# Two branch projections moved from the attention loop into the gate stage, and the values as a Strassen product

## The chip, the cores and the metric

The kernel runs on one core of one Trainium2 chip. The metric is the device time of one execution in microseconds; the median of three runs of the kernel before is 1399.12 us (1399.05 to 1400.21).

## What is computed

A decoder block for x of 1024 positions by 1024 channels, float32. The part that matters here, cut from the reference:

```python
h = rmsnorm(x, attn_norm_g[l])
z = h @ w_in[l]                          # u, v (512) | pooling (256) | q, k (1024) | values (512)
gates = jax.nn.sigmoid(h @ w_gate[l] + b_gate[l])      # 3 x 1024 columns
y_a = gmlp_mixer(z[..., :o_a], ...)      # layer norm of v, spatial gating, 256 channels
y_b = pool_mixer(z[..., o_a:o_b], ...)   # causal means over 2, 4, 8, 16 positions, 256 channels
y_c = diff_attn_mixer(...)               # 4 heads, two softmaxes each, 512 channels
merged = g_a * (y_a @ proj_a[l]) + g_b * (y_b @ proj_b[l]) + g_c * (y_c @ proj_c[l])
x = x + merged @ w_out[l]
x = x + conv_ffn(rmsnorm(x, ffn_norm_g[l]), w_up[l], conv_w[l], conv_b[l], w_down[l])
return rmsnorm(x, final_norm_g)
```

## The kernel before

Each float32 operand is split into a high part (a cast, L96 on ScalarE) and a low part (a subtraction, L97 on VectorE), both of a type that TensorE multiplies in one pass, and each product of two operands is three matmuls, high by low, high by high and low by high (`mm3`, L187 to L190). L189 is the line of nearly all matmuls. An activation is held as eight tiles of 128 channels by 1024 positions.

Most projections go through `strassen_pair` (L251 to L289): two output tiles of 128x1024, F1 and F2, from seven products (Strassen in Winograd's form) of 12 matmuls of 128x512 each, 84 in place of 96. `prepare` (L224) loads the weights and forms the operand sums on POOL; `winograd` (L209) forms the sums of the activation. Each result is an add on VectorE of a PSUM bank and a copied partial result (L260). The argument `mid` is called at four points of a pair, so that other work may be put between its products. The PSUM pool p1 has six banks with the tag "b" for these products and two with the tag "m" (`pm1`) for small work.

The stages in order, with their times in the profile:

- 0 to 61 us: RMS norm and the projections u and v.
- 61 to 118 us: `values` (L496), eight groups of 48 matmuls of 128x256, with `layer_norm`, `gating` and the `winograd` sums of h written between them.
- 118 to 200 us: one pair for the pooling branch, zb, and pairs for q and k of heads 0 to 2. `pooling` (L529) works on zb in steps that are called from the `mid` of the pairs; `pool_out` (L572) is a small matmul on its result. `times_r` (L347) multiplies a tile by the row factors RB, on POOL unless told otherwise. `store_qk` splits and stores q and k.
- 200 to 448 us: twelve gate pairs (loop at L689). Of each result POOL does `times_r`, ScalarE the sigmoid (L694), and the tile is stored to g_d.
- to 455 us: the pair of the last head's q and k.
- 455 to 604 us: attention, a loop over 32 tiles (head, block of 128 queries) in four steps that work on tiles t to t-3: scores (L677, L678, PE) with a running maximum (L680, VectorE), the exponential (L686, ScalarE), `combine` of the two softmaxes (L1003 to L1005, VectorE), transposition (L1020, PE), its copy (L1021, ScalarE) and the product with the values (L1029, PE). The generator `merge_ab` (L1086) is the filler of this loop: in each tile one group of 12 matmuls (mm<-yv,ph), a projection of y_a or y_b, and its product on VectorE with the sigmoid gate, read back from g_d as ga or gb (L1096). `load_p` splits the projection weights ph, `load_yab` the tiles yv.
- 604 to 1398 us: `merge_c`, the output projection, the FFN, the last norm.

A tile scheduler sets the order of the instructions of each engine from a simulated timeline when the program is built; each engine runs its queue in that order. SBUF tiles come from pools of a fixed number of buffers: a4 (34), w4 (13), c2 (6).

## Time and profile before

| What | us |
|---|---|
| median of three runs | 1399.12 |
| profiled execution | 1400.12 |
| its span on the core | 1398.4 |
| PE busy | 1349.2 (96%) |
| VectorE (DVE) busy | 958.0 (69%) |
| ScalarE (ACT) busy | 646.3 (46%) |
| GpSimd (POOL) busy | 516.8 (37%) |
| mean granted TensorE clock | 0.991 |

A busy time is a sum over the whole span; what a change in one stage is worth is read from the windows of that stage. A group of instructions in a view reads: line, engine, operation, tile written <- tiles read, form, count, then busy time and mean length, then the idle time of the engine before them and who ended it.

### The profile page before, as it was taken

To read this page: it belongs to the slowest core of one execution; us is meant where nothing else is said; L and a number is where in the kernel's file an instruction comes from. 1 tells how busy PE (TensorE), PEld (TensorE's weight loads), DVE (VectorE), ACT (ScalarE), POOL (GpSimd) and SP (SyncE) were. 2 spreads that over 40 slices of the span, in tenths; PEclk is the share of its full clock that TensorE was granted. 3 is DMA by queue.
4 is the path that set the end of the run, shared out by engine and by line. 5 is a ranking of instruction groups with operands and counts; after the bars stand their busy time and mean duration, and the time that the engine had idled before them with its cause. 6 is when DMAs were issued, how large, how long until landed. Compare 5 with 4: busy or idle time off the path is not lost.

```text
span 1398.4 us, 17778 instructions
## 1 busy us (share of the span) xinstructions
PE 1349.2 (96%) x6502; PEld 1126.8 (81%) x6502; DVE 958.0 (69%) x1464; ACT 646.3 (46%) x1105; POOL 516.8 (37%) x333
## 2 busy tenths in 40 slices
PE   8999999999999889999999999999999999999996
PEld 7898778888887678878777888888888887878786
DVE  7654766444454789967869677666777668985854
ACT  8542335343334567732666343433433435455461
POOL 0023376465552100012231566666666640102014
PEclk9999999999999999999999999999999999999998
DMA  6432235233338898497795222222222247845853
GB/s 204 131 97 77 76 151 181 91 120 106 113 114 233 254 239 233 130 268 180 207 229 121 91 75 90 78 74 90 90 76 90 81 161 271 286 120 152 224 129 121
DMA packets 79407, 204.65 MB, mean 146 GB/s; under 512 B 8334, under 2 KB 17678, under 8 KB 79320
## 3 DMA queue, kind: packets, MB, share of 16 engines
q1 hardware_dynamic: 67800, 180.44, 39.3%
q0 software_dynamic: 11520, 23.07, 9.5%
q8 instruction: 51, 0.84, 0.3%
q14 instruction: 36, 0.29, 0.1%
HBM read 143.70 MB, written 47.46 MB: 137 GB/s over the span
## 4 chain that ended last, share of the span: by engine, by line
PE 66%; DMA 11%; DVE 11%; issue 4%; ACT 3%; POOL 2%; SPq 0%; DVEq 0%; POOLq 0%; ACTq 0%
PE b L189 59%; PE mm L189 2%; DMA fr<-in_w_out 2%; DMA x<-in_xT 2%; PE ms L1029 1%; DMA fr<-in_w_down 1%; DVE fw L97 1%; DMA r<-in_w_gate 1%; DVE Sl L97 1%; DMA qs<-qk_d 1%; DMA pr<-in_w_proj 1%; POOL F L349 1%; DMA ssb<-sq 1%; DVE ft L97 1%; PE at L1020 1%
## 5 line engine op out<-in xcount | busy, mean ns | idle before, releaser
L189 PE MATMUL b<-ft,fw 128*128 128x512 f32 (+1 forms) x1308 | 291.8, 383 | 8.8 <-DVE fw L97 3.1
L189 PEld LDWEIGHTS b<-ft,fw 128*128 128x128 f32 x1308 | 238.9, 188 | 59.0 <-DVE fw L97 4.4
L349 POOL TENSOR_TENSOR F<-F,RB 128x1024 f32<-128x1024 f32 x74 | 205.3, 2777 | 135.3 <-DVE F L260 133.5
L189 PE MATMUL b<-hb,Ah 128*128 128x512 f32 x608 | 189.0, 390 | 0.0
L260 DVE TENSOR_TENSOR F<-b,c 128x512 f32<-128x512 f32 x152 | 100.6, 682 | 99.8 <-ACT c L279 46.5
L189 PE MATMUL b<-T,Sh 128*128 128x512 f32 x504 | 155.7, 389 | 2.0 <-ACT c L270 2.0
L97 DVE TENSOR_TENSOR Sl<-s,Sh 128x1024 fp32r<-128x1024 f32 x76 | 118.1, 1554 | 28.7 <-ACT Sh L96 20.8
L232 POOL TENSOR_TENSOR s<-r 128x512 f32<-128x512 f32 x36 | 56.7, 1576 | 207.4 <-DMA r<-in_w_up 83.4
L189 PEld LDWEIGHTS b<-hb,Ah 128*128 128x128 f32 x608 | 114.0, 188 | 23.9 <-issue 0.5
L97 DVE TENSOR_TENSOR Al<-r,Ah 128x1024 fp32r<-128x1024 f32 x38 | 51.6, 1358 | 102.7 <-issue 75.5
L189 PE MATMUL b<-hb,Al 128*128 128x512 f32 x304 | 118.4, 389 | 2.5 <-DVE Al L97 2.5
L96 ACT CAST Sh<-s 128x1024 fp32r<-128x1024 f32 x76 | 80.0, 1052 | 72.2 <-PE b L189 46.3
L189 PEld LDWEIGHTS b<-T,Sh 128*128 128x128 f32 x504 | 94.6, 188 | 21.9 <-ACT c L270 2.4
L189 PE MATMUL b<-hb,Sh 128*128 128x512 f32 x304 | 95.1, 394 | 4.0 <-DVE F L260 4.0
L189 PE MATMUL b<-T,Sl 128*128 128x512 f32 x252 | 98.1, 389 | 0.0
L96 ACT CAST Ah<-r 128x1024 fp32r<-128x1024 f32 x38 | 39.9, 1050 | 108.1 <-PE b L189 108.1
L96 ACT CAST fw<-fr 128x512 fp32r<-128x512 f32 x90 | 54.9, 623 | 62.2 <-DVE fw L97 26.3
L189 PE MATMUL b<-Tl,Sh 128*128 128x512 f32 x204 | 79.4, 389 | 0.0
L189 PE MATMUL b<-Th,Sl 128*128 128x512 f32 x204 | 78.7, 390 | 0.1
L189 PE MATMUL b<-Th,Sh 128*128 128x512 f32 x204 | 78.6, 389 | 0.0
L189 PE MATMUL b<-wh,hb 128*128 128x256 f32 x384 | 71.9, 286 | 1.9 <-ACT vg L425 1.9
L189 PEld LDWEIGHTS b<-hb,Sh 128*128 128x128 f32 x304 | 57.6, 190 | 16.9 <-DVE F L260 4.9
(250 smaller groups left out, 2802.6 us busy)
## 6 DMA issues: line engine op xcount, KB each, us to landing
fr<-in_w_down SPq DMA_DIRECT2D x47, 512.0 KB, 4.0
r<-in_w_up SPq DMA_DIRECT2D x42, 512.0 KB, 3.5
r<-in_w_gate SPq DMA_DIRECT2D x24, 512.0 KB, 3.8
g_d<-F SPq DMA_DIRECT2D x24, 512.0 KB, 2.6
act_d<-cv SPq DMA_DIRECT2D x22, 512.0 KB, 2.6
act<-act_d SPq DMA_DIRECT2D x22, 512.0 KB, 6.9
fr<-in_w_out SPq DMA_DIRECT2D x18, 512.0 KB, 5.7
ssb<-sq POOLq DMA_DIRECT2D x24, 256.0 KB, 3.9
```

The source lines that it names most:

```text
L96: nc.scalar.copy(hi, src)
L97: (eng or nc.vector).tensor_tensor(out=lo, in0=src, in1=hi.bitcast(F32), op=ALU.subtract)
L189: nc.tensor.matmul(ps, lhsT=w[a], rhs=x[b], start=first and i == 0, stop=last and i == 2, skip_group_check=more)
L232: eng.tensor_tensor(out=s1[:, :NH], in0=a21, in1=a22, op=ALU.add)
L260: nc.vector.tensor_tensor(out=o, in0=ps, in1=c, op=ALU.add)
L349: (eng or nc.gpsimd).tensor_tensor(out=F, in0=F, in1=RB, op=ALU.mult)
L1020: nc.tensor.transpose(pt[:, b * P:(b + 1) * P], st[t]["pr"][0][:, (4 * g + b) * P:(4 * g + b + 1) * P], ident)
L1029: nc.tensor.matmul(po[:, :P], lhsT=AH[t][:, kb, :], rhs=H["V"][:, kb, :], start=kb == 0, stop=kb == i)
```

## The change

Four things change.

- The values become one Strassen product: seven products of 48 matmuls of 128x256 where there were eight groups of 48. All `winograd` sums of h are formed ahead of it, the weights are loaded raw, and their sums and splits are made on VectorE and ScalarE between the products.
- `gating` and `pool_out` are tied in the order to the last matmul written before them; `pooling` takes two steps per `mid` and is finished within the first q/k pair; `pool_out` goes into the third. `times_r` of q and k of heads 0 to 2 goes to VectorE.
- The projections of branches a and b leave attention. `branch` computes them for gate pair n in the `mid`s of pair n+1, for the eight pairs of gates a and b, into the two "m" banks, and multiplies by the sigmoid tile in SBUF; F2 comes before F1. g_d then holds products, and `load_mg` reads and sums two of them with an accumulating DMA, from tile 20 of attention on. The attention loop has no filler; scores get four PSUM banks instead of three.
- `start` in the third part of `strassen_full` runs under a raised priority, and five of the eight scalings in the tail read PSUM instead of a copy.

```diff
-    def load_V(c):
-        return [list(load_parts(w_tm[1 + c, j].rearrange("p a b -> p (a b)"), 2, True))[0] for j in range(2)]
+    def load_V():
+        r = [[w4(n="wr") for _ in range(2)] for _ in range(2)]
+        for c, k in ((0, 0), (0, 1), (1, 0), (1, 1)):
+            nc.sync.dma_start(out=r[c][k], in_=w_tm[1 + c, k].rearrange("p a b -> p (a b)"))
+        return r
...
-    def values(c, gs):
...
+    def values():
+
+        (a11, a12), (a21, a22) = w_V
...
+        def prod(banks, w, tn, first, more):
+            for t in range(4):
+                for j in range(4):
+                    x, y = [o[:, t * P:(t + 1) * P] for o in h.T[j][tn]], wsl(w, j, 256)
+                    dst = banks[t // 2][:, t % 2 * 256:t % 2 * 256 + 256]
...
+                        mm3(dst, x, y, False, j == 3, True)
...
+        def store(o, banks, c, r, i):
+
+            for b in range(2):
+                TT(out=o[b], in0=banks[b], in1=c[b], op=ALU.add)
+                for t in range(2):
+                    sl = o[b][:, t * 256:(t + 1) * 256]
+                    nc.scalar.mul(sl, sl, R8[:, 4 * i + 2 * b + t:4 * i + 2 * b + t + 1])
...
+        A11, A12 = operand(a11), operand(a12)
+        b1, b2 = ([pb1() for _ in range(2)] for _ in range(2))
+        prod(b1, A11, "B11", True, True)
+        c1 = copies([c2("v") for _ in range(2)], b1)
+        yield
+        s1, s2 = w4(n="s1"), w4(n="s2")
+        TT(out=s1, in0=a21, in1=a22, op=ALU.add)
+        TT(out=s2, in0=s1, in1=a11, op=sub)
+        prod(b2, A12, "B21", True, False)
+        store(c1, b2, c1, 0, 0)
+        S1 = operand(s1)
+        yield
+        b3 = [pb1() for _ in range(2)]
+        prod(b3, S1, "T1", True, True)
+        S2 = operand(s2)
+        TT(out=a21, in0=a11, in1=a21, op=sub)
+        TT(out=a12, in0=a12, in1=s2, op=sub)
+        yield
+        prod(b1, S2, "T2", False, True)
+        k2 = copies(wide("c2"), b1)
+        S3 = operand(a21)
+        yield
+        prod(b1, S3, "T3", False, True)
+        k3 = copies(wide("c3"), b1)
+        store([c2("v") for _ in range(2)], b3, k3, 1, 1)
+        A22 = operand(a22)
+        yield
+        b4 = [pb1() for _ in range(2)]
+        prod(b4, A22, "T4", True, False)
+        store(k3, b4, k3, 1, 0)
+        S4 = operand(a12)
+        yield
+        prod(b3, S4, "B22", False, True)
+        store(k2, b3, k2, 0, 1)
...
+            with tc.issue_after(last_mm[0].ins):
+                for c in range(2):
+                    ch = 2 * g + c
+                    nc.tensor.matmul(pv[:, c], lhsT=vg[ch // 4][:, ch % 4, f * P:(f + 1) * P],
...
-    values(0, (2, 3))
-    h.winograd(xt, 0)
+    for j in range(4):
+        h.winograd(xt, j)
+    vs = values()
+    next(vs)
     layer_norm()
-    values(1, (2, 3))
-    h.winograd(xt, 1)
-    values(0, (0, 1))
-    h.winograd(xt, 2)
+    for _ in range(4):
+        next(vs)
     gating(0)
-    values(1, (0,))
+    next(vs)
     gating(1)
-    h.winograd(xt, 3)
     wB = prepare(w_qk[0])
-    values(1, (1,))
+    next(vs)
     zb = strassen_pair(wB, h, pb1)
...
+    def pool_outs():
+        for f in range(2):
+            yield
+            with tc.issue_after(last_mm[0].ins):
+                pool_out(f, zb[f])
+
     for i in range(NHEAD - 1):
         ops = prepare(w_qk[1 + i])
         if i == 0:
             pl = pooling(zb)
-        store_qk(i, strassen_pair(ops, h, pb1, lambda: next(pl, None)))
+        store_qk(i, strassen_pair(ops, h, pb1, lambda: (next(pl, None), next(pl, None))), nc.vector)
+        if i == 0:
+            for _ in pl:
+                pass
+        if i == 1:
+            pl = pool_outs()
+
     for _ in pl:
         pass
-
-    def pool_outs():
-        for f in range(2):
-            for _ in range(2):
-                yield
-            pool_out(f, zb[f])
-
-    po_ = pool_outs()
...
+    def load_y(i):
+
+        alloc = a4 if i % 2 == 0 else w4
+        hi, lo = alloc([P, 2, NH], F32R, "yv"), alloc([P, 2, NH], F32R, "yv")
+        for j in range(2):
+            raw = c2("yr")
+            nc.sync.dma_start(out=raw, in_=y_d[i, :, half(j)])
+            split(hi[:, j, :], lo[:, j, :], raw)
+        return [(hi[:, j, :], lo[:, j, :]) for j in range(2)]
+
+    def load_branch(n):
+
+        m, g = 2 * n % 8, 2 * (n // 4)
+        raw = c2("pr")
+        nc.sync.dma_start(out=raw.rearrange("p (m a b) -> p m a b", m=2, a=2),
+                          in_=w_proj[m:m + 2, :, g:g + 2, :].rearrange("m p a b -> p m a b"))
+        hl = w4([P, 2, NH], F32R, "ph")
+        split(hl[:, 0, :], hl[:, 1, :], raw)
+        return hl[:, 0, :], hl[:, 1, :]
+
+    def branch(n, Fs, whl, yb):
+
+        for k in (1, 0):
+            F = Fs[k]
+            for j in range(2):
+                ps = pm1()
+                for ki in range(2):
+                    mm3(ps, wsl(whl, 2 * k + ki), yb[ki][j], ki == 0, ki == 1)
+                nc.vector.tensor_tensor(out=F[:, half(j)], in0=ps, in1=F[:, half(j)], op=ALU.mult)
+                if j == 1:
+                    nc.sync.dma_start(out=g_d[2 * n + k], in_=F)
+                yield
+
+    br = iter(())
     for n_ in range(12):
-        Fs = strassen_pair(w_gate[n_], h, pb1, lambda: next(po_, None))
-        for k, F in enumerate(Fs):
+        if n_ in (0, 4):
+            yb = [load_y(2 * (n_ // 4) + i) for i in range(2)]
+        if n_ < 8:
+            whl = load_branch(n_)
+        Fs = strassen_pair(w_gate[n_], h, pb1, lambda: next(br, None))
+        for _ in br:
+            pass
+        for k, F in reversed(list(enumerate(Fs))):
             m = 2 * n_ + k
             times_r(F)
             nc.scalar.activation(out=F, in_=F, func=AF.Sigmoid, bias=col(C_BG + m), scale=1.0)
-            nc.sync.dma_start(out=g_d[m], in_=F)
+            if n_ >= 8:
+                nc.sync.dma_start(out=g_d[m], in_=F)
+        br = branch(n_, Fs, whl, yb) if n_ < 8 else iter(())
...
+                    with tc.high_priority():
+                        start(d, 1, B[0][d])
...
-    score_bank[0], pat, pms, pmm = pt2("sc", 3), pt2("at", 2), pt2("ms", 1), pt2("mm", 2)
+    score_bank[0], pat, pms, pmm = pt2("sc", 4), pt2("at", 2), pt2("ms", 1), pt2("mm", 1)
...
-    mg = []
...
+    mg = {}
+
+    def load_mg(m):
+
+        if m < KT and m not in mg:
+            mg[m] = a4(n="mg")
+            nc.sync.dma_start(out=mg[m], in_=g_d[m])
+            accumulate(mg[m], g_d[8 + m])
...
-        if t >= 1:
-            next(filler, None)
...
-        if t >= 29:
-            pre_c(t - 29)
+        if t >= 20:
+            load_mg(t - 20)
+        if t >= 27:
+            pre_c(t - 27)
...
-                scale_out(k, 0, sl, RB[:, sl], nc.gpsimd if k <= (2, 0)[q] else nc.vector)
+                if k <= (2, 0)[q]:
+                    scale_out(k, 0, sl, RB[:, sl], nc.gpsimd)
+                else:
+                    scale_out(k, 0, sl, pb[:, :n], nc.vector)
```

**Order of PE at the end of a gate pair.** b_2200 (before) and b_2064 (after) are the last product, S4, of a pair; yv and ph are the operands of a projection, hb, Th, Tl, Ah, Sh, Sl and A those of the pairs; m_2307 is the first group of the projection for F1 of the pair before. Before:

```order
L189 MATMUL b_2316<-Tl_838,Sh_2305 128x512
L189 MATMUL b_2200<-hb_346,Sh_2181 128x512 [waits DVE_49]
L189 MATMUL b_2200<-hb_346,Sh_2181 128x512
L189 MATMUL b_2200<-hb_346,Sl_2182 128x512
L189 MATMUL b_2200<-hb_349,Sh_2181 128x512 x2
L189 MATMUL b_2200<-hb_349,Sl_2182 128x512
L189 MATMUL b_2200<-hb_352,Sh_2181 128x512 x2
L189 MATMUL b_2200<-hb_352,Sl_2182 128x512
L189 MATMUL b_2200<-hb_355,Sh_2181 128x512 x2
L189 MATMUL b_2200<-hb_355,Sl_2182 128x512
L189 MATMUL b_2316<-Th_837,Sl_2306 128x512
```

Now:

```order
L191 MATMUL b_2064<-hb_352,Sl_2046 128x512
L191 MATMUL b_2064<-hb_355,Sh_2045 128x512 x2
L191 MATMUL b_2064<-hb_355,Sl_2046 128x512
L191 MATMUL m_2307<-yv_1865,ph_2021 128x512 [waits DVE_49]
L191 MATMUL m_2307<-yv_1866,ph_2021 128x512
L191 MATMUL m_2307<-yv_1865,ph_2021 128x512
L191 MATMUL m_2307<-yv_1875,ph_2021 128x512
L191 MATMUL m_2307<-yv_1876,ph_2021 128x512
L191 MATMUL m_2307<-yv_1875,ph_2021 128x512
L191 MATMUL m_2329<-yv_1865,ph_2021 128x512 [waits DVE_49]
```

The last product was followed and preceded by matmuls of the next pair; now it is followed by two groups of a projection, which wait for VectorE.

**Order of DVE at the same place.** F_331 and F_328 (before), F_328 and F_324 (now) are results of pairs; L794 is the product of a projection with its gate. Before:

```order
L260 TENSOR_TENSOR F_331_2256<-b_2200,c_2254 128x512 [waits Activation_49]
L260 TENSOR_TENSOR F_331_2256<-b_2258,c_2254 128x512 [waits PE_49]
L260 TENSOR_TENSOR F_348_2358<-b_2359,c_2329 128x512 [waits DMAHW0_49,PE_49,Activation_49]
L97 TENSOR_TENSOR Al_2433<-r_353_2422,Ah_2432 128x1024 [waits DMAHW7_49,Activation_49]
L260 TENSOR_TENSOR F_328_2227<-b_2200,c_2225 128x512 [waits PE_49]
L97 TENSOR_TENSOR Sl_2437<-s_355_2426,Sh_2436 128x1024 [waits Activation_49,Pool_49]
L97 TENSOR_TENSOR A_361_2440<-r_354_2423,A_361_2440 128x512 [waits DMAHW0_49,Activation_49]
```

Now:

```order
L262 TENSOR_TENSOR F_328_2137<-b_2064,c_2135 128x512 [waits DMAHW6_49,Activation_49]
L262 TENSOR_TENSOR F_328_2137<-b_2147,c_2135 128x512 [waits PE_49]
L97 TENSOR_TENSOR ph_2189<-pr_2187,ph_2189 128x512 [waits DMAHW4_49,Activation_49]
L262 TENSOR_TENSOR F_324_2099<-b_2064,c_2089 128x512 [waits PE_49]
L794 TENSOR_TENSOR F_328_2137<-m_2259,F_328_2137 128x512 [waits Activation_49]
L794 TENSOR_TENSOR F_328_2137<-m_2282,F_328_2137 128x512
L97 TENSOR_TENSOR Al_2203<-r_334_2192,Ah_2202 128x1024 [waits DMAHW5_49,Activation_49]
L794 TENSOR_TENSOR F_324_2099<-m_2307,F_324_2099 128x512 [waits PE_49,Activation_49]
L794 TENSOR_TENSOR F_324_2099<-m_2329,F_324_2099 128x512 [waits DVE_49,PE_49]
```

The products with the gate, which empty the banks of m_2259 and m_2282, stand behind the add that reads the end of S4.

**Order of DVE in the values stage.** wl is the low part of a weight operand: wl_916 of S1, wl_970 of S2, wl_1027 of S3. There was no such row in the stage before; the layer norm and the Tl splits stood alone:

```order
L522 TENSOR_SCALAR vg_123<-vg_123,mv,rs_123_868 128x256 [waits DVE_49]
L522 TENSOR_SCALAR vg_123<-vg_123,mv,rs_123_868 128x256 x3
L522 TENSOR_SCALAR vg_124<-vg_124,mv,rs_123_868 128x256 x4
L527 TENSOR_TENSOR vg_123<-vg_123,wk_533 128x1024 [waits DVE_49]
L527 TENSOR_TENSOR vg_124<-vg_124,wk_533 128x1024 [waits DVE_49]
L527 TENSOR_TENSOR vg_123<-vg_123,wk_533 128x1024 [waits DVE_49]
L527 TENSOR_TENSOR vg_124<-vg_124,wk_533 128x1024 [waits DVE_49]
L97 TENSOR_TENSOR Tl_1007<-x_90,Th_1006 128x1024 [waits PE_49,Activation_49]
```

Now, the rows up to the split of S2, then those of the layer norm up to the split of S3:

```order
L97 TENSOR_TENSOR Tl_720<-x_87,Th_719 128x1024 [waits Activation_49]
L564 TENSOR_TENSOR wr_494<-wr_494,s_133_856 128x1024 [waits DVE_49]
L97 TENSOR_TENSOR wl_916<-s_132_855,wh_915 128x1024 [waits PE_49,Activation_49]
L536 TENSOR_TENSOR v_800<-b_750,v_800 128x512 [waits DMAHW0_49,PE_49]
L97 TENSOR_TENSOR Tl_725<-x_91,Th_724 128x1024 [waits Activation_49]
L591 TENSOR_SCALAR va_829<-mv 128x8 [waits DVE_49]
L97 TENSOR_TENSOR wl_970<-s_133_856,wh_969 128x1024 [waits PE_49,Activation_49]
```

```order
L131 SCALAR_TENSOR_TENSOR rs_130_831<-rs_131_832,rs_130_831 128x8 [waits DVE_49]
L595 TENSOR_SCALAR vg_123<-vg_123,mv,rs_130_831 128x256 [waits DVE_49]
L595 TENSOR_SCALAR vg_123<-vg_123,mv,rs_130_831 128x256 x3
L595 TENSOR_SCALAR vg_124<-vg_124,mv,rs_130_831 128x256 x4
L600 TENSOR_TENSOR vg_123<-vg_123,wk_501 128x1024 [waits DVE_49]
L600 TENSOR_TENSOR vg_124<-vg_124,wk_501 128x1024 [waits DVE_49]
L97 TENSOR_TENSOR wl_1027<-wr_495,wh_1026 128x1024 [waits Activation_49]
```

The splits of operands that PE waits for have moved in between the work of the layer norm.

**Order of DVE in the q/k stage.** Al is the low part of the first operand of the next pair, F_180 and F_201 (before), F_183 and F_186 (now) are zb. Before, the rows up to the Al split:

```order
L542 TENSOR_TENSOR pw_1498<-F_180_1371 128x1023
L260 TENSOR_TENSOR F_201_1501<-b_1502,c_1469 128x512 [waits PE_49,Activation_49]
L541 COPY pw_1516<-pw_1498 64x2 [waits DVE_49]
L542 TENSOR_TENSOR pw_1516<-pw_1498 64x1022
L541 COPY pw_1555<-F_183_1400 128x1
L542 TENSOR_TENSOR pw_1555<-F_183_1400 128x1023
L546 TENSOR_TENSOR h_206_1536<-pw_1516,cs 128x16 [waits DVE_49,Activation_49]
L547 TENSOR_TENSOR h_206_1536<-h_206_1536,F_180_1371 128x16 [waits DVE_49]
L548 SCALAR_TENSOR_TENSOR F_180_1371<-pw_1516,cs,F_180_1371 128x1024 [waits DVE_49]
L550 COPY F_180_1371<-h_206_1536 128x16 [waits DVE_49]
L97 TENSOR_TENSOR Al_1596<-r_213_1585,Ah_1595 128x1024 [waits DMAHW0_49,Activation_49]
```

Now, the rows up to the Al split:

```order
L621 SCALAR_TENSOR_TENSOR F_183_1338<-pw_1468,cs,F_183_1338 128x1024 [waits DVE_49]
L614 COPY pw_1531<-pw_1514 64x8 [waits DVE_49]
L615 TENSOR_TENSOR pw_1531<-pw_1514 64x1016
L623 COPY F_183_1338<-h_207_1487 128x16 [waits DVE_49]
L262 TENSOR_TENSOR F_210_1509<-b_1438,c_1507 128x512 [waits DMAHW5_49,Activation_49]
L262 TENSOR_TENSOR F_210_1509<-b_1517,c_1507 128x512 [waits PE_49]
L619 TENSOR_TENSOR h_215_1535<-pw_1531,cs 128x16 [waits DVE_49]
L351 TENSOR_TENSOR F_210_1509<-F_210_1509,RB 128x1024 [waits DVE_49]
L620 TENSOR_TENSOR h_215_1535<-h_215_1535,F_186_1367 128x16 [waits DVE_49]
L621 SCALAR_TENSOR_TENSOR F_186_1367<-pw_1531,cs,F_186_1367 128x1024 [waits DVE_49]
L97 TENSOR_TENSOR Al_1578<-r_220_1567,Ah_1577 128x1024 [waits DMAHW4_49,Activation_49]
```

Before, the Al split stood thirteen rows behind the add into F_180 that ends a pair; now it stands twenty-five rows behind the add into F_183, with three more sums of pooling, one more difference and one more scaling in front of it.

## Rows read from the trace of the kernel before

**Rows 1.** Page: span, and busy time of each engine with its share and instructions.
```profile
span 1398.4 us, 17778 instructions
...
PE 1349.2 (96%) x6502; PEld 1126.8 (81%) x6502; DVE 958.0 (69%) x1464; ACT 646.3 (46%) x1105; POOL 516.8 (37%) x333
```

**Rows 2.** Windows by stage: stretch, its us, busy us of each engine, granted clock, DMA.
```profile
61.50:118.34 56.84, 56.84 (x450) 55.98 (x450) 34.45 (x73) 20.37 (x33) 16.46 (x13) 1.00 0.35 112
118.34:200.00 81.66, 76.51 (x334) 62.10 (x333) 55.53 (x55) 27.73 (x35) 38.60 (x20) 1.00 0.28 100
200.00:448.00 248.00, 247.94 (x1091) 204.28 (x1090) 119.46 (x105) 99.53 (x122) 130.90 (x75) 1.00 0.40 131
455.00:604.00 149.00, 137.34 (x829) 117.41 (x828) 128.14 (x403) 97.13 (x285) 8.58 (x9) 0.97 0.80 214
```

**Rows 3.** Windows of 20 us, the same columns.
```profile
300.00:320.00 20.00, 20.00 (x90) 16.57 (x89) 8.52 (x8) 7.83 (x11) 9.76 (x7) 1.00 0.38 127
80.00:100.00 20.00, 20.00 (x169) 20.00 (x168) 6.29 (x7) 7.54 (x11) 5.14 (x4) 1.00 0.12 42
...
540.00:560.00 20.00, 19.67 (x134) 16.89 (x132) 19.20 (x63) 14.10 (x40) 0.86 (x1) 1.00 0.94 243
...
580.00:600.00 20.00, 19.75 (x142) 18.00 (x140) 19.10 (x74) 14.81 (x49) 0.86 (x1) 1.00 0.46 118
```

**Rows 4.** Groups of instructions, forms apart: busy us, mean ns, idle us before.
```profile
L260 DVE TENSOR_TENSOR F<-b,c 128x512 f32<-128x512 f32 x152 | 100.6, 682 | 99.8 <-ACT c L279 46.5 <-PE b L189 26.8 <-issue 26.4
L97 DVE TENSOR_TENSOR wl<-wr,wh 128x1024 fp32r<-128x1024 f32 x4 | 4.9, 1220 | 5.2 <-ACT wh L96 5.2
L349 POOL TENSOR_TENSOR F<-F,RB 128x1024 f32<-128x1024 f32 x74 | 205.3, 2777 | 135.3 <-DVE F L260 133.5 <-ACT RB L148 1.7
L694 ACT ACTIVATE F<-F,cs 128x1024 f32<-128x1024 f32 x24 | 27.7, 1154 | 61.8 <-POOL F L349 61.4
```

**Rows 5.** Timeline of DVE, 72 to 77 us: start, length, line, operation.
```profile
72.77 0.17 DVE L131 SCALAR_TENSOR_TENSOR rs<-rs,rs 128x8 f32<-128x8 f32 x1
72.97 2.68 DVE L522 TENSOR_SCALAR vg<-vg,mv,rs 128x256 f32<-128x256 f32 x8
75.57 2.36 DVE L527 TENSOR_TENSOR vg<-vg,wk 128x1024 f32<-128x1024 f32 x2
```

**Rows 6.** Waits of PE, 118 to 200 us: total, times, longest.
```profile
PE m L575 <- issue: 2.6, 1, 2.6
PE b L189 <- DVE Al L97: 2.5, 1, 2.5
```

**Rows 7.** Timelines of PE and DVE in the q/k stage.
```profile
118.34 0.63 PE L189 MATMUL b<-hb,Ah 128*128 128x512 f32 x2
...
145.32 0.69 DVE L260 TENSOR_TENSOR F<-b,c 128x512 f32<-128x512 f32 x1 [5.45 <-PE b L189]
```

**Rows 8.** Timeline of PE, 484 to 488 us; in brackets the wait before.
```profile
485.73 2.55 PE L189 MATMUL mm<-yv,ph 128*128 128x512 f32 x6 [1.99 <-DVE ga L1096]
```

**Rows 9.** Timeline of DVE, 481 to 487 us.
```profile
484.98 0.69 DVE L1096 TENSOR_TENSOR ga<-mm,ga 128x512 f32<-128x512 f32 x1 [3.44 <-DMA ga<-g_d]
485.59 0.28 DVE L680 CUSTOM_DVE_ANT_0 sc<-sc,T 128x128 f32<-128x128 f32 x1
```

**Rows 10.** Groups of PE, 455 to 604 us.
```profile
L189 PE MATMUL mm<-yv,ph 128*128 128x512 f32 x186 | 52.0, 417 | 6.5 <-ACT ph L96 4.0 <-DVE ga L1096 2.5
```

**Rows 11.** Groups of DVE, 455 to 604 us.
```profile
L1096 DVE TENSOR_TENSOR ga<-mm,ga 128x512 f32<-128x512 f32 x16 | 11.0, 686 | 5.6 <-DMA ga<-g_d 3.4 <-PE mm L189 1.9
L1096 DVE TENSOR_TENSOR gb<-mm,gb 128x512 f32<-128x512 f32 x15 | 10.3, 685 | 2.2 <-DMA gb<-g_d 1.8 <-PE mm L189 0.4
...
L97 DVE TENSOR_TENSOR ph<-pr,ph 128x512 fp32r<-128x512 f32 x12 | 8.2, 686 | 1.2 <-ACT ph L96 1.2
...
L97 DVE TENSOR_TENSOR yv<-yr,yv 128x1024 fp32r<-128x1024 f32 x2 | 3.1, 1534 | 2.8 <-ACT yv L96 2.8
```

**Rows 12.** Window of 3 us in attention, columns as in rows 2.
```profile
486.00:489.00 3.00, 3.00 (x9) 2.27 (x9) 1.21 (x4) 1.21 (x7) 0.00 (x0) 0.53 1.02 217
```

97 lines of the change are left out of this document (37 added, 60 removed).

## The prediction

> **What bounds the kernel now.** I read the page's totals first [rows 1]: TensorE (PE) is busy 1349.2 of 1398.4 us, so any matmul put where PE has no gap costs its own length, and the kernel can be sped up only by fewer matmuls or by closing the 49 us of gaps. The windows by stage [rows 2] tell where those gaps are. The values stage and the gate stage have none (56.84 of 56.84, 247.94 of 248.00). The q/k stage has 5.15 us, the attention stage 11.7 us. Attention differs in a second way: VectorE (DVE) is busy 128.14 of 149.00 there, 86%, PE only 92%, and the granted clock is 0.97 instead of 1.00. So attention is a stage in which two engines are nearly full, and the gate stage one in which DVE has half its time free (119.46 of 248). The short windows [rows 3] give PE's pace: 90 matmuls of 128x512 in 20.00 us, 0.222 us each, and 169 of 128x256, 0.1185 us each. They also show how full DVE gets late in attention, 19.20 and 19.10 of 20 us, 96 and 95.5%.
>
> The profiled execution took 1400.12 us, 1.0 over the median of the three runs; I add to it and take the 1.0 off at the end. About 0.2%, 2.8 us, is what a measurement of this kernel can tell from no change.
>
> **Values.** 384 matmuls of 128x256 become 336: 48 x 0.1185 = -5.7 us where PE has no gap. The rest of the work moves to DVE: four sums and subtractions and seven splits, each like the 128x1024 split of a raw tile at 1.22 us [rows 4], and eight adds out of PSUM at 0.68 us. They hide as long as DVE is ahead of PE. Two places in its queue say that it is not. The split of S1 stands behind two weight sums, four BN_AGGR groups and several Tl splits. Walking the queue with 1.22 us per 128x1024 row from the free point near 63.4, S1 is ready at about 78.4, and PE, after two products of 48, comes at 76.9: 1.5 us. The split of S3, wl_1027 in the order piece for DVE in values, stands behind the layer norm: ten small steps that follow each other by 0.20 us (2.0), eight TENSOR_SCALAR (2.68) and two products with the gain (2.36) [rows 5]. It is ready at about 92.5 and PE comes at 89.3: 3.2 us. So -5.7 + 1.5 + 3.2 = **-1.0 us**. Ends: -5.7, both waits covered; +4, each wait twice as long.
>
> **Pooling and q/k.** The stage's gaps are two waits [rows 6]: 2.6 us at a pool_out matmul that stood in PE's queue before its input was there, and 2.5 us for an Al split. Pinning pool_out to a later pair removes the first. The second gets longer: pooling now goes in one lump, and the order piece for DVE in q/k shows the Al split at its end, 25 rows behind the add into F_183 with times_r on DVE among them. That add started 27.0 us into the pair that computes it (145.32 against 118.34 [rows 7]); eleven rows of about 1.22 (13.4), four adds (2.7) and ten small rows at 0.17 (1.7) make 17.8 us, of which I take off 2 to 3 for starts that overlap the end before; so Al is there at 42 to 43 us. PE has 168 matmuls of 0.222 us, 37.3 us, until it needs it: a wait of 5.2 us. Net -5.15 + 5.2 = **0.0 us**; ends -4 (the lump slips in where DVE waits) and +3.
>
> **Gate stage, the projections.** 16 matmul groups of 12, 192 in all, move into a stage without a gap: 192 x 0.222 = **+42.7 us**, with no bound below that since PE is busy 247.94 of 248.00. Their other work hides: 32 products of 0.68 us, 8 splits of ph and 8 of y on DVE come to some 33 us, and DVE has 128 free; the DMAs (the same bytes as before, earlier) go into a stage at share 0.40. POOL keeps the scaling by RB at 2.777 us and ScalarE the sigmoid at 1.154 [rows 4].
>
> **Gate stage, a new wait.** The order pieces for PE show what decides here. Before, the twelve matmuls of S4 that end a pair stand between matmuls of the next pair, which need nothing from it. Now they are followed directly by m_2307, a projection that needs one of the two "m" banks. That bank is freed by the product F_328 <- m_2259 on DVE, and in DVE's queue this product stands right behind the add F_324 <- b_2064, which waits for the end of those same S4 matmuls. So PE stops until DVE has done an add and a product: 0.68 + 0.68 [rows 4], and two handoffs. A handoff from DVE is read in attention [rows 8, 9]: the product at 484.98 lasts 0.69 to 485.67, and PE starts at 485.73. With 0.06 each way this is 1.48 us, and I take 1.5. The sigmoid of F_328 is needed too: its last add can start 24 matmuls (5.3 us) before the end of S4, and 0.68 + 2.78 + 1.15 us are done 0.7 us before it, so it is not the later one. The same pattern stands at seven boundaries of pairs (0 to 6). At one of them, where the operands of b replace those of a, one more 1.22 us split stands ahead of the product: 2.9. Sum 6 x 1.5 + 2.9 = **+11.9 us**; ends 8 (each one product and one handoff less) and 18 (POOL slows the sigmoid and each wait grows by 1).
>
> **Attention without filler.** PE loses 186 matmuls in this window [rows 10], at 0.222 us 41.3 us, which leaves at most 96 and, without the half-clock stretches, about 91. DVE loses the filler's products, 11.0 + 10.3, eight of the twelve ph splits, 5.5, and two y splits, 3.1 [rows 11]: 29.9 us. Starts overlap the end before by 0.08 (485.59 against 485.67 [rows 9]), times 41 instructions 3.3, so 128.1 - 29.9 + 3.3 = 101.5 us remain. ScalarE had 97.13 [rows 2] and loses splits too. DVE is then the fullest engine and sets the floor, 101.5. It will not be reached: the loop still goes from scores to maximum, exponential, combination and transposition across four engines, and its windows near the end had DVE at 96 and 95.5%. At 95% this is 107. The stage takes 149.0 now: **-42.0 us**. Ends: -47.5 (the floor) and -31 (118, below). What the filler gave to attention was cover: PE worked on it while it waited for DVE.
>
> **The rest.** The tail's first scalings read PSUM and save one ScalarE copy of the last chain, -0.4 us. In the block behind merge_c and in the FFN the order of the instructions is the same, names apart, so the raised priority costs and gives nothing; loading the sum of the two products with an accumulating DMA replaces the accumulation of gb into ga and is issued from tile 20 on, long before it is needed.
>
> **Sum.** -1.0 + 0.0 + 42.7 + 11.9 - 42.0 - 0.4 = +11.2 on 1400.1: 1411.3, and 1.0 less on the median: **1410.3 us**.
>
> The Trainium skill has a rule that speaks against this change. In attention PE, which had been busy with short gaps, stood for 1.99 us before 485.73 [rows 8], and the stretch 486 to 489 behind it ran at a granted clock of 0.53, most of it at the 1.2 GHz level of the two [rows 12]. "TensorE: Matmul & The Clock Gate", section "HAM oscillation — how this bites in real kernels", says that a loop in which PE waits for its operands every round can fall back to the slow clock in every round. The trace bears it out in part: gaps of 2.6 and 2.5 us in the q/k stage [rows 6] left that stage's clock at 1.00 [rows 2]. By the rows the clock costs nothing in my sum, since DVE is the limit; by that rule attention would go PE-bound, the third rival.
>
> **Rivals.**
> 1. *The new waits hide* (faster). All the waits that I read from the order, 11.9 at the boundaries, 4.7 in values and 5.2 in q/k, depend on DVE being behind PE. If DVE gets to these instructions earlier than my walk says, up to 21.8 us go: 1388.5. It decides from 14.0 us on (11.2 + 2.8). For it: DVE is half idle in all three stages. Against: the boundary wait is one engine waiting for the other's answer, and no speed of DVE removes it. Chance 0.17.
> 2. *Attention at its DVE floor, values without waits* (no change): -5.5 and -4.7 from the forecast, 1400.1. For it: 7.8 us of DVE's idle time in attention stands ahead of the filler's own products [rows 11]. Against: no window shown is fuller than 96%. Chance 0.15.
> 3. *The clock falls in attention* (slower still): a stretch of 3 us at 0.53 loses 1.4 us of PE's work. PE needs 91; one such stretch in 19 of the 32 tiles makes 118, over DVE's 107: 1421. For it: PE will be idle 15% of the stage, in short pieces. Against: the q/k stage's two gaps left the clock at full. Chance 0.13.
> 4. *The change does not do what it says*: the scheduler could have put the projections elsewhere. The order shows them between the products of the next pair, so this is out, but for the priority, which does nothing.
>
> **Chances.** The forecast has the remaining 0.55, with a range of its own from 1403 to 1417. Faster by over 0.2%: rival 1 and a little of the second, 0.18. Within: 0.17. Slower: the forecast and the third, 0.65. The range holds 8 in 10 if it cuts the outer half of rivals 1 and 3: 1393 to 1420.
>
> **What would show it.** Right: the gate stage about 303 us long, with some seven waits of PE of 1.5 us at projections <- DVE products; attention about 107 us, DVE over 90% busy; two PE waits for wl splits in values; one of about 5 us for Al in q/k. Wrong: a gate stage of 291 with no waits (rival 1), attention at or below 102 (rival 2), attention over 115 with a clock below 0.95 (rival 3).

## The result and the profile after

The kernel after the change takes 1462.38 us, the median of four runs (1459.54 to 1463.22), beside 1399.09 for the kernel before in the same comparison (1397.28 to 1400.21). The ratio is 1.0451 (95% interval 1.0434 to 1.0468): **63 us slower**, 52 above the forecast of 1410.3 and 42 above the upper end of the range.

First the totals of the page of the kernel after, which answer to [rows 1]:

```profile
span 1460.7 us, 17671 instructions
...
PE 1370.3 (94%) x6454; PEld 1137.1 (78%) x6454; DVE 954.2 (65%) x1485; ACT 650.8 (45%) x1114; POOL 504.4 (35%) x327
```

48 matmuls are gone, as the values should have it, and yet PE is busy 21 us longer, and stands for 90 us instead of 49. Where this is, the windows tell. They are cut at events that both kernels have: the first matmul of the pair for zb, the first matmul of a score, the last one of a score, and the last matmul of all. Before:

```profile
118.34:444.36 326.02, 320.82 (x1406) 263.37 (x1405) 174.99 (x159) 124.20 (x153) 168.16 (x94) 1.00 0.37 122
...
444.36:595.63 151.27, 139.29 (x830) 119.18 (x828) 124.03 (x380) 97.11 (x271) 12.31 (x11) 0.97 0.82 219
...
595.63:1390.67 795.04, 777.14 (x3510) 642.22 (x3508) 577.53 (x761) 360.99 (x575) 316.56 (x205) 1.00 0.49 143
```

After (columns as in [rows 2]; the last row is a piece of 4.55 us in the gate stage, which is read further below):

```profile
116.77:544.92 428.15, 386.72 (x1594) 310.56 (x1593) 191.77 (x215) 131.81 (x169) 161.31 (x90) 0.95 0.30 103
544.92:668.91 123.99, 101.91 (x660) 87.36 (x659) 99.32 (x342) 89.47 (x261) 13.04 (x12) 0.96 0.89 220
668.91:1453.51 784.60, 772.60 (x3491) 640.11 (x3490) 572.77 (x758) 360.24 (x575) 316.33 (x204) 1.00 0.48 143
...
275.45:280.00 4.55, 4.54 (x13) 3.59 (x14) 2.67 (x3) 1.31 (x2) 4.55 (x4) 0.62 0.28 115
```

| Stretch | before | after | difference | predicted |
|---|---|---|---|---|
| to the first pair (values) | 118.34 | 116.77 | -1.6 | -1.0 |
| q/k and gates | 326.02 | 428.15 | **+102.1** | +54.6 |
| from the first score to the end | 946.31 | 908.59 | -37.7 | -42.4 |

So the miss is in one place. In the q/k and gate stretch PE stands for 41.4 us (428.15 less 386.72) instead of 5.2, and is busy 65.9 us longer, though the moved matmuls were worth 42.7. The granted clock fell there from 1.00 to 0.95. The waits of PE over the whole span of the kernel after say who ended the idle time (total, times, longest):

```profile
PE b L191 <- DVE F L262: 20.2, 11, 5.5
PE m L191 <- DVE F L794: 17.3, 7, 3.4
PE m L191 <- ACT yv L96: 5.7, 1, 5.7
```

The second row is the predicted wait, at seven boundaries, but 2.3 to 3.4 us each instead of 1.5 to 2.9. The first row holds a wait at the same boundaries that the prediction does not have at all: seven of 1.40 to 1.46 us, beside one of 5.5 and one of 2.0 (read below) and two behind 550 us. One boundary shows both. These are rows of the timeline of the kernel after, 268 to 286 us: start, length, engine, line, operation, and in brackets the engine's idle time before and its releaser.

```profile
268.26 0.39 PE L191 MATMUL b<-Th,Sl 128*128 128x512 f32 x1
268.74 0.59 ACT L281 COPY c<-b 128x512 f32<-128x512 f32 x1 [6.49 <-PE b L191]
...
269.36 1.29 DVE L262 TENSOR_TENSOR F<-b,c 128x512 f32<-128x512 f32 x2 [5.36 <-ACT c L281]
...
270.11 0.74 PE L191 MATMUL b<-hb,Sh 128*128 128x512 f32 x2 [1.46 <-DVE F L262]
...
270.73 2.77 POOL L351 TENSOR_TENSOR F<-F,RB 128x1024 f32<-128x1024 f32 x1 [18.82 <-DVE F L262]
...
273.20 0.69 DVE L262 TENSOR_TENSOR F<-b,c 128x512 f32<-128x512 f32 x1 [1.96 <-PE b L191]
273.53 1.15 ACT L811 ACTIVATE F<-F,cs 128x1024 f32<-128x1024 f32 x1 [3.69 <-POOL F L351]
...
274.59 1.03 ACT L96 CAST Ah<-r 128x1024 fp32r<-128x1024 f32 x1
274.71 1.29 DVE L794 TENSOR_TENSOR F<-m,F 128x512 f32<-128x512 f32 x2 [0.82 <-ACT F L811]
...
275.45 4.56 PE L191 MATMUL m<-yv,ph 128*128 128x512 f32 x12 [2.29 <-DVE F L794]
...
282.67 2.88 PE L191 MATMUL m<-yv,ph 128*128 128x512 f32 x12
```

Three things are to be seen.

- **The first wait, 1.46 us.** S4 is accumulated onto a bank that DVE must first read for F2. That add needs the copy c of the product T3, which ends directly before S4. So PE ends T3 (268.65), ScalarE copies it (to 269.33), DVE adds (to 270.04), and PE goes on at 270.11. The kernel before has this wait too, once, in the pair of the last head, behind which no next pair follows:

```profile
451.36 0.73 PE L189 MATMUL b<-hb,Sh 128*128 128x512 f32 x2 [1.40 <-DVE F L260]
```

- **The second wait, 2.29 us.** Its product at 274.71 waits for the sigmoid, not for the last add (273.20 to 273.89). The sigmoid's chain starts with the two adds at 269.36 and goes over POOL (2.77) and ScalarE (1.15) to 274.68, 1.5 us after PE is done with S4.
- **The clock.** The twelve matmuls behind the two waits take 4.56 us; twelve of the same kind take 2.88 at 282.67. The window from 275.45 to 280 had a granted clock of 0.62, most of it at 1.2 GHz. The other boundaries are alike: twelve take 4.37 to 4.61 us, and eighteen 5.99 at the one where b replaces a.

The row of the Ah cast (274.59) tells why PE had nothing else: the operands of the next pair stand behind the sigmoid on ScalarE. Their raw weights were not late: the loads were issued at 253.67 and 254.76, and such loads land 3.3 to 10.1 us after their issue in this trace. Before, the next pair's matmuls lay around S4 and covered the same dependences.

The third row of the waits is the first use of yv. It stands at an eighth boundary, between the last q/k pair and the first gate pair: the scheduler put a projection ahead of that pair's first product. The 2.0 us in the first row are the wait before S4 at the same boundary. These are rows of PE there:

```profile
204.50 0.89 PE L191 MATMUL b<-hb,Sh 128*128 128x512 f32 x2 [1.98 <-DVE F L262]
...
214.85 1.32 PE L191 MATMUL m<-yv,ph 128*128 128x512 f32 x2 [5.75 <-ACT yv L96]
```

The 5.5 us in the first row are the q/k wait that the prediction expected at Al; these rows of DVE and POOL in the kernel after show pooling in front of the add that frees the bank:

```profile
151.43 2.31 DVE L621 SCALAR_TENSOR_TENSOR F<-pw,cs,F 128x1024 f32<-128x1024 f32 x1
...
152.62 2.24 POOL L236 TENSOR_TENSOR s<-r,r 128x512 f32<-128x512 f32 x1
...
153.77 1.12 DVE L614 COPY pw<-pw 64x8 f32<-64x8 f32 x1
154.80 1.21 DVE L615 TENSOR_TENSOR pw<-pw 64x1016 f32<-64x1016 f32 x1
154.82 2.31 POOL L235 TENSOR_TENSOR s<-s,r 128x512 f32<-128x512 f32 x1
156.04 1.12 DVE L623 COPY F<-h 128x16 f32<-128x16 f32 x1
157.08 1.27 DVE L262 TENSOR_TENSOR F<-b,c 128x512 f32<-128x512 f32 x2
```

### The profile page after: what moved, and what is told of

It is laid out like the page before. It is cut to its first block, busy times and chain, and to the rows that moved or that the text cites. A ratio compares the mean times of both kernels' runs of the same rounds, so it can differ in the third digit from the quotient of the medians.

```text
span 1460.7 us, 17671 instructions
## 1 busy us (share of the span) xinstructions
PE 1370.3 (94%) x6454; PEld 1137.1 (78%) x6454; DVE 954.2 (65%) x1485; ACT 650.8 (45%) x1114; POOL 504.4 (35%) x327
## 4 chain that ended last, share of the span: by engine, by line
PE 63%; issue 13%; DVE 12%; DMA 6%; POOL 3%; ACT 2%; SPq 0%; DVEq 0%; POOLq 0%; ACTq 0%
PE b L191 59%; PE m L191 2%; DMA kl<-qk_d 1%; DVE sc L757 1%; DMA pr<-in_w_proj 1%; DMA fr<-in_w_down 1%; POOL F L351 1%; DVE fw L97 1%; POOL s L234 1%; DVE sc L1125 1%; DVE F L262 1%; POOL mg L104 1%; DMA mg<-gc 1%; DVE ft L97 1%; DMA act<-act_d 1%
## 5 line engine op out<-in xcount | busy, mean ns | idle before, releaser
L351 POOL TENSOR_TENSOR F<-F,RB 128x1024 f32<-128x1024 f32 x68 | 187.1, 2753 | 232.7 <-DVE F L262 212.7
L262 DVE TENSOR_TENSOR F<-b,c 128x512 f32<-128x512 f32 x152 | 100.8, 682 | 187.5 <-PE b L191 95.7
L234 POOL TENSOR_TENSOR s<-r 128x512 f32<-128x512 f32 x36 | 62.3, 1729 | 190.9 <-DMA r<-in_w_up 84.3
L97 DVE TENSOR_TENSOR Al<-r,Ah 128x1024 fp32r<-128x1024 f32 x38 | 56.2, 1478 | 91.9 <-issue 76.7
L97 DVE TENSOR_TENSOR Sl<-s,Sh 128x1024 fp32r<-128x1024 f32 x76 | 97.1, 1278 | 21.6 <-ACT Sh L96 17.4
L191 PE MATMUL m<-yv,ph 128*128 128x512 f32 x192 | 61.0, 476 | 23.9 <-DVE F L794 17.3
L96 ACT CAST fw<-fr 128x512 fp32r<-128x512 f32 x90 | 54.6, 622 | 57.8 <-DVE fw L97 23.6
```

The costliest lines, as they stand in the source:

```text
L96: nc.scalar.copy(hi, src)
L97: (eng or nc.vector).tensor_tensor(out=lo, in0=src, in1=hi.bitcast(F32), op=ALU.subtract)
L191: last_mm[0] = nc.tensor.matmul(ps, lhsT=w[a], rhs=x[b], start=first and i == 0, stop=last and i == 2, skip_group_check=more)
L234: eng.tensor_tensor(out=s1[:, :NH], in0=a21, in1=a22, op=ALU.add)
L262: nc.vector.tensor_tensor(out=o, in0=ps, in1=c, op=ALU.add)
L351: (eng or nc.gpsimd).tensor_tensor(out=F, in0=F, in1=RB, op=ALU.mult)
```

## The experiments

**The halves apart.** The first half is the kernel before with the Strassen values, the lump of pooling, the pinned matmuls and `times_r` on DVE, and with the filler kept. The second is the kernel before with the moved projections and the attention of the change. The fourth point of the change, the priority and the scalings in the tail, stands in neither. The edits against the kernel after, at the place where they part:

```diff
 e_first_half
-        Fs = strassen_pair(w_gate[n_], h, pb1, lambda: next(br, None))
+        Fs = strassen_pair(w_gate[n_], h, pb1)
...
+            next(filler, None)
 e_second_half
...
-    vs = values()
-    next(vs)
+    values(0, (2, 3))
+    h.winograd(xt, 0)
```

> The kernel before with only the first half of the change: Strassen values, pooling in one lump, pool_out and gating pinned, times_r of q and k on DVE; projections stay in attention as filler. By the trace of the changed kernel: values 1.6 us shorter, q/k stage 2 us more idle and 5 us lost to half clock behind the 5.5 us wait, so about 1403 to 1404. If these waits came from the projections' loads and not from this half: 1396 to 1398.

> The kernel before with only the second half: projections of a and b in the gate stage, attention without filler; values, pooling and pool_out as before. Theory A: the waits at the pair ends belong to this half, so the time is that of the changed kernel less the 5 us of the first half: 1455 to 1458. Rival C (pooling and pool_out, which no longer fill the gate stage's start and shift the DVE queue, are what makes the boundaries bare): 1410 to 1420, near the time that was predicted.

Measured: first half 1392.89, ratio 0.9973 (0.9951 to 0.9996); second half 1457.79, ratio 1.0425 (1.0390 to 1.0459). Relative to the 1397.75 of this comparison that is -4.9 and +60.0, together +55 beside the 63 of the whole; the 8 us between are not accounted for (the stretch of the q/k and gate pairs alone is 420.65 us in the second half, 428.15 in the whole). Almost all the loss is in the second half, and the first half is a small gain of its own. The expectation for it, 1403 to 1404, missed. Its 5.5 us wait is there, and its stretch of q/k and gates is 2.6 us longer than before (328.64), but its profiled execution is 3.1 us shorter up to the first pair and 7.0 behind the last score, and no run shows why the latter.

**Attention alone.** The kernel before, with the loop of the change and without any projection of a and b.

```diff
-        if t >= 1:
-            next(filler, None)
...
+        if t >= 20:
+            load_mg(t - 20)
```

> The kernel before with attention as in the changed kernel but without any projection of a and b: it leaves out these projections and their products, and sums the two sigmoid tiles instead. Gate stage as before. If the attention loop's length in the changed kernel (124 us from the first score to the last, 151 before, and 11 us less behind it) is its own: 1399 - 27 - 11 = 1361 us, VectorE under 85% busy in the loop. If it is long there because its loads come late (5.8 us of waits for kh and kl): 1350 to 1355 us, and the loop near the 107 us that was predicted.

Measured: 1358.58, ratio 0.9725 (0.9696 to 0.9754), 39.2 us less, where the prediction had 42.0. The window of the loop (first to last score), and one that answers to the last of [rows 2], without the filler:

```profile
441.37:561.84 120.47, 101.56 (x656) 86.32 (x655) 98.83 (x344) 89.33 (x263) 13.26 (x12) 0.97 0.90 225
453.00:564.00 111.00, 93.49 (x621) 79.82 (x620) 96.53 (x340) 86.34 (x265) 8.72 (x9) 0.97 0.93 237
```

The stage takes 111 us (like the row of before, the window ends some 2 us behind the first matmul of `merge_c`), near the 107 of the prediction, but no engine is full in it: DVE is busy 87%, PE 84%, ScalarE 78%. The waits of this window go round between PE, DVE and ScalarE, so I take the loop to be held by its chain across the engines; no run tests that. And the clock is at 0.97, as in the loop before: a PE that stands for a sixth of the time did not lose more of it here.

**What holds PE at the boundaries.** The first experiment keeps the projections behind the matmuls written before them, since one theory was that the scheduler puts them too early.

```diff
-                for ki in range(2):
-                    mm3(ps, wsl(whl, 2 * k + ki), yb[ki][j], ki == 0, ki == 1)
+                with tc.issue_after(last_mm[0].ins):
+                    for ki in range(2):
+                        mm3(ps, wsl(whl, 2 * k + ki), yb[ki][j], ki == 0, ki == 1)
```

> The changed kernel with one edit: each projection group of branch is tied behind the matmul written before it, so the scheduler can't put it a pair early. Theory A (the projections of a pair's own F2 run early in that pair and hold both m banks until its sigmoid, so at the pair's end PE has nothing it may start): the two waits per pair, 1.45 us at S4 and 2.3 us at a projection, go, and with them the half-clock stretch behind each; eight times 3.75 idle and 1.7 of lost clock are 43 us, so about 1420 us and a gate stage with less than 10 us of PE idle. Rival B (the projections' tiles take buffers from the pool that holds the pairs' operands, so that the next pair is prepared late): waits stay and move to the first product of a pair, waiting for an Ah or Al split; 1450 us or more.

Measured: 1474.31, ratio 1.0552 (1.0509 to 1.0594), some 12 us above the kernel after. The waits of PE in it, 110 to 510 us:

```profile
PE b L191 <- ACT Ah L96: 22.1, 8, 7.1
PE b L191 <- DVE Al L97: 15.0, 8, 3.5
```

The waits for the product are gone, and PE waits longer, for the operands of the next pair: it stands for 48.3 us in the stretch instead of 41.4, as rival B said. So the place that the scheduler gave to the projections is not what costs: held to the written order, PE finds the next pair not ready.

Two experiments then take operands away whose loads and splits stand in the way: all of yv and ph, or ph alone. Parts of h are used in their place.

```diff
 e_lent
-            yb = [load_y(2 * (n_ // 4) + i) for i in range(2)]
+            yb = [[h.b[i][j] for j in (0, 0)] for i in range(2)]
 e_lent, e_ph_lent
-            whl = load_branch(n_)
+            whl = h.b[2][0]
```

> The changed kernel with the projections of a and b taken on tiles that lie in SBUF anyway (slices of hb in place of yv and ph): as many matmuls and products as before, but no loads, no splits and no buffers for yv and ph. It leaves out the true operands of these projections. Theory B (the waits at the pair ends come from the preparation of the next pair, for which the tiles yv and ph take 3 to 4 of the 13 buffers): the waits go, the gate stage costs its 42.7 us of matmuls and little more; 1398 less 4 (first half) less 39 (attention) plus 43: about 1398 us, up to 1405. If the waits come from the product of F2 and the m banks alone, they stay: 1440 us or more.

> As the run with both operands lent, but yv is loaded, split and kept as in the changed kernel; only ph is lent (it leaves out the true weights of the projections). If ph, which is loaded once per pair just ahead of prepare, is what pushes the preparation back: near the run with both lent, within 10 us, but for the boundary between pairs 3 and 4 where yv changes. If the four buffers of yv do it: 1440 us or more.

Measured: e_lent 1405.28, ratio 1.0039 (1.0014 to 1.0065); e_ph_lent 1423.57, ratio 1.0151 (1.0118 to 1.0183). The q/k and gate stretch of e_lent:

```profile
116.99:486.66 369.67, 364.77 (x1594) 299.81 (x1593) 189.17 (x199) 122.75 (x152) 149.54 (x90) 1.00 0.31 108
```

All matmuls, products and stores are there as in the kernel after; PE's idle time falls from 41.4 to 4.9 us and the clock is back at 1.00. With ph alone lent, one boundary of the seven still has its wait (2.0 us), and the wait for yv stays; the time lies between the two that were expected. So the dependences at a boundary cost nothing as such; they cost where the next pair's operands are late, and the loads and splits of yv and ph help to make them late. Whether that is by the w4 buffers that they hold or by their place in the queues, these two runs do not tell apart.

The next shows whether the order alone is enough. It leaves all loads and buffers as they are, and writes `prepare` of the next pair into the fourth `mid` of the running one. A second one adds the pin of e_pin.

```diff
-        Fs = strassen_pair(w_gate[n_], h, pb1, lambda: next(br, None))
...
+        def mid():
+            calls[0] += 1
+            next(br, None)
+            if calls[0] == 4 and n_ < 11:
+                nxt_.append(prepare(w_gate[n_ + 1]))
+
+        Fs = strassen_pair(ops_ if n_ else w_gate[0], h, pb1, mid)
+        ops_ = nxt_[0] if nxt_ else None
```

> The changed kernel with prepare of the next gate pair (loads, sums, splits) written into the fourth mid of the pair before, instead of behind its sigmoids and behind the loading of ph; nothing else. In the order the first product of the next pair then stands ahead of S4 again, and a projection with it. Theory B: the 1.45 us waits at S4 and most of the 2.3 us waits go, and the half clock with them: 1400 to 1412 us. If buffers alone decide (as many tiles as before are alive), little changes: over 1445 us.

> As the run with prepare ahead, and the projections tied behind the matmul written before them, as in the run that tied them alone and took 1474 us. If the tie did harm only because the next pair was late, the two together are as fast as prepare ahead alone or some us faster, since the m banks are not held over a pair: 1395 to 1410. If holding them in program order costs by itself: 1415 or more.

Measured: e_ahead 1420.08, ratio 1.0111 (1.0060 to 1.0161); e_ahead_pin 1425.66, ratio 1.0170 (1.0134 to 1.0205). e_ahead is above its expectation, and e_ahead_pin falls on the side on which the tie costs by itself; but the intervals overlap, so that is not shown. The trace of e_ahead_pin has no wait at the seven boundaries either, and one of 10.1 us for Ah and one of 4.4 for Al at the eighth. In e_ahead the boundary has no wait; these rows of PE stand between matmuls without a bracket:

```profile
276.01 0.39 PE L191 MATMUL m<-yv,ph 128*128 128x512 f32 x1
...
276.24 0.62 PE L191 MATMUL b<-hb,Ah 128*128 128x512 f32 x2
```

Its window from the first pair to the first score, and the part of it from 235 us on:

```profile
120.67:506.54 385.87, 371.28 (x1597) 303.82 (x1596) 206.91 (x216) 133.75 (x168) 162.18 (x90) 0.97 0.33 114
...
235.00:506.54 271.54, 271.54 (x1200) 224.84 (x1199) 136.64 (x139) 96.60 (x118) 129.09 (x71) 1.00 0.32 107
```

PE's waits in it from 110 to 510 us (total, times, longest):

```profile
PE b L191 <- DVE F L262: 7.5, 2, 5.5
PE m L191 <- ACT yv L96: 6.2, 1, 6.2
PE m L191 <- DVE yv L97: 0.9, 1, 0.9
```

No row of the kind m <- F is left, and F L262 is down to two waits, neither at a boundary between moved pairs: the lump of pooling (5.5 us) and one at the eighth boundary (2.0 us), which this edit does not reach. From 235 us to the first score PE has no idle time and the clock is 1.00; the 0.97 of the whole window comes from the part in front, where the waits are left. The sigmoid's chain is about as long (4.9 us from the add at 264.93, against 5.3) and is now covered. This shows that the order in which the next pair's operands are made is enough to remove the boundary's cost, with no buffer freed; it does not show that the buffers played no part in making them late. Of the 42.3 us that the stretch gets shorter, 26.8 are idle time and 15.4 are PE's busy time, that is the clock. What is left of the stretch's idle time, 14.6 us, and the lower clock stand in front, at places that this edit leaves as they were.

**What is left, mended.** Three kernels take the rest away: pooling goes back to one step per `mid` (in the first half alone, e_first_pool1); the move with that, with `prepare` ahead, and with a gate pair of branch c put before each group of four so that yv has time to come (e_move_mended); and the same with branch a alone moved, b as filler in every second tile and three banks for scores as before (e_half_filler).

```diff
 e_first_pool1, e_move_mended, e_half_filler
-        store_qk(i, strassen_pair(ops, h, pb1, lambda: (next(pl, None), next(pl, None))), nc.vector)
+        store_qk(i, strassen_pair(ops, h, pb1, lambda: next(pl, None)), nc.vector)
...
 e_move_mended
-    for n_ in range(12):
+    for q_, n_ in enumerate((8, 0, 1, 2, 3, 9, 4, 5, 6, 7, 10, 11)):
...
 e_half_filler
...
-        if n_ < 8:
+        if n_ < 4:
             whl = load_branch(n_)
...
+    filler = merge_b()
```

> The first half of the change alone, with one edit: pooling goes one step per mid, as in the kernel before, over two q/k pairs. In DVE's order the Al split of the next pair then stands twelve rows behind the add into F_183 instead of twenty-five. If the lump of pooling rows is what made PE wait 5.5 us in the first q/k pair (and lose some 3 us at half clock behind it), that wait goes: 5 to 8 us under the first half alone, which took 0.9973 of the kernel before, so 0.992 to 0.994, about 1389 us. If the wait comes from times_r on DVE or the order of the adds, it stays at 0.997.

> The whole change with its waits mended: prepare one pair ahead, pooling one step per mid, and two gate pairs of branch c put in front of the pairs of a and of b, so that yv is split before it is needed. What is left is the move itself: first half 0.992 to 0.994 of before, attention -39 us, gate stage +42.7 us of matmuls: 0.994 to 0.998, 1390 to 1397 us. If other waits take the place of the mended ones: over 1405 us.

> As the mended version, but only the projections of branch a go into the gate stage (four pairs); those of branch b stay in attention as filler, one group in every second tile. Attention without filler had 19 to 22 us of PE idle in a loop of 120 to 124 us, about as much as the 96 matmuls of branch b take (21.3 us). If the filler's worth is the idle time it covers, half the filler is nearly free: 10 to 15 us under the mended version, 1378 to 1387 us, faster than both kernels. If VectorE paces the loop, the filler's products (16 x 0.69 and splits, about 17 us) lengthen it by as much as the gate stage saves: 1390 to 1397 us.

Measured: e_first_pool1 1389.70, ratio 0.9941 (0.9924 to 0.9958); e_move_mended 1404.89, ratio 1.0051 (1.0032 to 1.0070); e_half_filler 1402.59, ratio 1.0036 (1.0022 to 1.0049). e_first_pool1 beats both kernels. The windows from the first pair to the first score, and of the attention loop, in e_first_pool1:

```profile
115.22:439.43 324.21, 320.60 (x1406) 263.39 (x1405) 177.55 (x171) 124.83 (x154) 149.14 (x90) 1.00 0.37 126
439.43:588.04 148.61, 136.52 (x830) 117.04 (x828) 124.92 (x380) 97.15 (x271) 12.32 (x11) 0.99 0.81 222
```

In e_move_mended:

```profile
116.59:483.89 367.30, 363.69 (x1596) 299.24 (x1595) 202.59 (x216) 133.76 (x168) 161.09 (x90) 1.00 0.36 121
483.89:608.37 124.48, 102.83 (x658) 87.53 (x656) 99.06 (x341) 89.69 (x262) 13.25 (x12) 0.96 0.87 220
```

And in e_half_filler:

```profile
118.93:464.88 345.95, 342.34 (x1502) 281.52 (x1501) 193.03 (x195) 130.45 (x162) 156.22 (x90) 1.00 0.36 124
464.88:602.31 137.43, 121.93 (x738) 102.27 (x736) 111.50 (x365) 95.54 (x271) 12.36 (x11) 0.98 0.89 240
```

The gate stage is nearly without gaps in all three (3.6 us of PE idle time in the stretch, clock 1.00), so these show what the move itself is worth. Against e_first_pool1 the moved matmuls cost 43.1 us of PE's time in the stretch with the gates (363.69 less 320.60); the loop gives 24.1 back and the part behind it 4.5. Half of them cost 21.7 and give 11.2 and 2.2. So about two thirds come back, 28.6 of 43.1 and 13.4 of 21.7. The rest had filled gaps: without the filler PE's busy time in the loop falls by 33.7 us, but its idle time there rises from 12.1 to 21.7. This is why mending the waits leaves a loss of 15 us, and the half move one of 13. Both expectations missed: that for the whole move took the loop to give 39 us back, and that for the half took the filler left in the loop to be nearly free, where it lengthens the loop by 13 us (124.48 to 137.43). Each of these parts is read from one execution, and executions of one kernel differ by some us: the runs of the kernel before in this comparison lie between 1394.09 and 1402.84.

## Why the prediction was wrong

- **Direction and place: right.** Slower, at the seven boundaries of the gate pairs, with attention not paying for the projections.
- **Values, -1.0: right in size**, -1.6, in part by luck. The two waits for wl splits came, with a third, at 0.8, 0.3 and 0.9 us: 2.0 together instead of 4.7. But the clock fell to 0.76 from 90 to 97 us, right behind them, and the 336 matmuls saved 3.9 us of PE's time (56.84 less 52.95) instead of 5.7. The window of the stage, which answers to the first of [rows 2]:

```profile
61.50:116.77 55.27, 52.95 (x396) 51.09 (x396) 45.82 (x75) 28.38 (x45) 10.49 (x11) 0.97 0.32 102
```

- **Pooling and q/k, 0.0: nearly right in size, by luck.** One wait of 5.5 us, against 5.2 predicted, but at the matmul S4 of that pair, whose bank the late add frees, and not at Al. The 2.0 us wait before S4 of the last q/k pair was not foreseen; e_first_half, with the same pooling and pool_out but no projection behind that pair, does not have it. And the clock lost some: e_first_half takes 328.64 us for the stretch and e_first_pool1 324.21, 4.4 us for the lump.
- **Projections, +42.7: right.** 43.1 where nothing waits.
- **"New wait", +11.9: wrong, the step that failed.** The idle time of the stretch grew by 36.2 us. (1) The prediction took the sigmoid's chain to begin 5.3 us before the end of S4. It does not: the first of the two adds waits for the copy of T3, and the second starts only 3.2 us before that end. So the sigmoid is the later one, and each wait is 2.3 us: 17.3 in all, near the upper end of 18. (2) The same copy makes PE wait before S4, about 1.4 us at seven boundaries, 10 us. The order piece for PE of the kernel before shows "waits DVE_49" at that matmul (the piece of the kernel after begins behind it), and the trace of before shows the bare wait once, 1.40 us at 451.36; the prediction looked at what follows S4 and not at what it waits for once nothing of the next pair stands before it. (3) The first use of yv, 6.6 us in two pieces at the eighth boundary, was put among the work that hides. That the operands of the next pair would come behind the sigmoid, which is what left the first two bare, was not asked.
- **"By the rows the clock costs nothing in my sum": wrong.** It was asked of attention alone. In the q/k and gate stretch PE's busy time is 386.72 with the waits and 363.69 in e_move_mended without: 23.0 us. At six of the seven boundaries the twelve matmuls behind the waits took 4.37 to 4.61 us, against 2.88, and at the seventh eighteen took 5.99. The Trainium skill's rule ("TensorE: Matmul & The Clock Gate", section "HAM oscillation — how this bites in real kernels"), that a loop in which PE waits every round can fall back to the slow clock in every round, is borne out here in kind, in the gate stage. In attention, where the prediction set it against the rows, little changed: 0.96 against 0.97 before. Over nine runs the loop's clock was 0.97 to 0.99 with the whole filler (before, e_first_half, e_first_pool1) and 0.93 to 0.97 without any (after, e_second_half, e_attn_bare, e_lent, e_ahead, e_move_mended), so there may be a small loss there too.
- **Attention and the rest, -42.4: nearly right against the kernel before** (-37.7), but not by the mechanism given: DVE is not at 95% (85% from 556 to 669 us, 87% in e_attn_bare), and against the better first half the loop returns 24.
- **Rivals.** The first, that the waits hide, had the right idea of what decides, and the wrong sign for this kernel: "no speed of DVE removes it" was not tested, but other work for PE does, as e_ahead shows. The third had the clock, in the wrong stage.

The misses of the q/k and gate stretch add up: 24.3 us more idle time than predicted (36.2 against 11.9; about 5.4 at the product, 10.1 before S4, 6.6 for yv, 2.3 in q/k) and 23.0 of clock, 47.3 of the 47.5 by which it missed.

## What to carry to other kernels

Work moved from a stage with gaps into a stage without costs its full length there and returns only the part that was not filling a gap, so price both by a run without the work before pricing any wait. When the order puts dependent work at the end of a block, list for each matmul there what it waits for and which matmul of the next block is ready then; a dependence as old as the kernel begins to cost when its cover goes. Make the next block's operands before the engines are given the tail of this one.
